# Gate and up projections of a hybrid decoder step as seven half products per pair of tiles, down projection in two parts

## Chip, cores and metric

The kernel runs on one NeuronCore of a Trainium2 chip. The core's engines are TensorE (PE, with its weight loads PEld), VectorE (DVE), ScalarE (ACT), GpSimd (POOL) and SyncE (SP, which issues the DMAs). The metric is the device time of one execution in microseconds.

## The reference

One inference step of a one-layer decoder: 512 prompt tokens and 8 sequences of 8 sampled tokens, 576 tokens together, 1,024 features. Two groups of token mixers (a state space model and an RWKV-7 recurrence) are followed by an output projection, then by the part that the change concerns, and by a per-layer embedding:

```
hf = rmsnorm(h, w['norm_ffn'])
h = h + (jax.nn.silu(hf @ w['w_gate']) * (hf @ w['w_up'])) @ w['w_down']
gate = jax.nn.sigmoid(rmsnorm(h, w['norm_ple']) @ w['w_ple_gate'])
h = h + gate * (p.astype(h.dtype) @ w['w_ple_proj'])
```

`rmsnorm` divides each token's row by its root mean square and multiplies by a weight per feature. The inner width D_FF is 2,816, which is 22 tiles of 128. All inputs are float32.

## The kernel before

Everything is kept transposed: features on the 128 partitions, the 576 tokens along the free dimension. `hs[c]` (c from 0 to 7) are the eight tiles of the residual h, each 128 x 576.

*Matmuls in three parts.* A float32 product is made from the faster format float32r: every operand is split into hi (a copy rounded by ScalarE, line 92 in `act`) and lo (the rest, a subtraction), and hi*hi + hi*lo + lo*hi is accumulated in PSUM (`mm3`, lines 208 to 212). `split` (line 177) does it for activations, `wsplit` (line 186) for weights; the subtractions go to GpSimd and VectorE in turn (line 195 for weights, line 183 for activations), unless `lo_eng` names an engine. One PSUM bank holds 512 columns, so a tile of 576 tokens is done in two halves of 288 (`HV`). `linear(xs, ps)` (line 214) loads the weights of one output tile in blocks of up to four k tiles (128 x 512, 256 KB, tag raw with three buffers), splits them and issues six matmuls per k tile. `lin_bank` hands out PSUM tiles of two banks from two pools with two tiles each.

*Order of the work.* The program lists the operations in order; a scheduler with a timeline of its own decides, per engine, in which order they are queued: the earlier in the program the higher the priority, but what is not ready in that timeline lets others go ahead. Each engine then runs its queue strictly in that order.

*Feed-forward stage (lines 1282 to 1312).* `after` (line 1251) multiplies each tile of h by the norm's weight, splits it into the operand `XF` (buffers xhi and xlo, eight of each), and adds up the squares. The normalisation by token, `rs` (128 x 576), comes from `rstd_of` (line 1262): sums over features by matmuls with a column of ones (line 306), square root and reciprocal, transposes on TensorE (line 312) and a copy by ScalarE. For each of the 22 inner tiles f, `linear` makes gate and up; line 1298 multiplies gate by rs, ScalarE applies Silu, line 1303 multiplies by up, and the result is split into `AF2[f]` (tags ah0 to ah21 and al0 to al21, one buffer each), lo on GpSimd. The factor rs of up is left out there and applied behind the down projection: for each of eight tiles of h, line 1308 makes the down product over all 22 inner tiles, line 1310 multiplies by rs on VectorE, line 1311 adds to h on GpSimd, and `after` prepares the next stage's operand and squares.

*Last stage (lines 1317 to 1363).* The per-layer gate (8 tiles, weights WP split once and kept) in two token ranges of 320 and 256 columns, its product with the embedding part `PL` (loaded from DRAM, `pl`), the addition to h and the final norm. WP and PL live in the buffers of `AF2`, whose tags they use.

## Time and profile before

| | us |
|---|---|
| median of the runs (3, from 1414.13 to 1415.24) | 1415.04 |
| the profiled execution | 1409.36 |
| its span, from the first to the last instruction | 1407.6 |
| token mixers and output projection, 0 to about 911 | 911 |
| gate and up, about 911 to 1195 | 284 |
| down, about 1195 to 1334 | 139 |
| per-layer gate and final norm, about 1334 to the end | 74 |

TensorE's mean granted clock over the span is 0.936 of full speed. In the rows of groups that follow, the fields are line, engine, operation, output<-inputs, shape and count, then busy time in us and the mean of one in ns, then the idle time of the engine just before them with what ended it. In timeline rows the first two numbers are start and length in us, and the bracket gives the idle time before and its releaser. In rows of stretches the columns are start and end, length, busy us (and instructions) of PE, PEld, DVE, ACT and POOL, the granted TensorE clock, and the share and GB/s of the DMA engines.

### The profile page before, as it was taken

The page shows a single profiled execution, that of the slowest core. Times are in us where ns is not written, and L with a number is a line of the kernel's source. Part 1 is how long each engine was busy: PE and PEld are TensorE (multiplying, and loading weights), DVE is VectorE, ACT ScalarE, POOL GpSimd, SP SyncE. Part 2 cuts the span into 40 slices and gives each one's busy share as a digit, 9 for nine tenths or more (in the row PEclk, how much of TensorE's full clock was granted, in tenths as well). Part 3 has the DMA queues.
Part 4 walks back from the last instruction along what each step waited for, and adds up shares of the span by engine and source line. Part 5 has one row for each costly group of instructions (what it writes and reads, how often), then busy time and mean ns, then how long its engine had stood idle before and what let it go on. Part 6 is the DMA issues. An engine that isn't in the chain of part 4 may idle for free.

```text
span 1407.6 us, 24774 instructions
## 1 busy us (share of the span) xinstructions
PE 1278.4 (91%) x9761; PEld 1188.2 (84%) x9761; DVE 721.8 (51%) x1335; ACT 590.8 (42%) x1186; POOL 565.4 (40%) x552
## 2 busy tenths in 40 slices
PE   6887999899889988969869987999999999999996
PEld 5786897788678967956748877999999999999996
DVE  6648658696777766845265574422222221122255
ACT  6564436544653464334534353332333333222253
POOL 4345515632543334123346574523332333344432
PEclk9998999999999988957969997999999999999998
DMA  4322233234223412342514541223233323332432
GB/s 157 128 56 81 73 109 99 68 92 119 61 84 86 114 50 88 117 117 101 194 64 140 179 127 45 84 82 83 83 83 83 83 83 83 83 82 82 126 109 68
DMA packets 94452, 135.46 MB, mean 96 GB/s; under 512 B 34704, under 2 KB 39056, under 8 KB 94336
## 3 DMA queue, kind: packets, MB, share of 16 engines
q1 hardware_dynamic: 94336, 133.88, 32.2%
q8 instruction: 77, 1.26, 0.4%
q14 instruction: 39, 0.32, 0.1%
HBM read 106.10 MB, written 27.75 MB: 95 GB/s over the span
## 4 chain that ended last, share of the span: by engine, by line
PE 67%; DVE 18%; DMA 5%; ACT 4%; issue 4%; POOL 1%; SPq 1%; DVEq 0%; ACTq 0%; POOLq 0%
PE lin L210 17%; PE lin L212 17%; PE lin L211 16%; PE lin L578 2%; DVE Tt L638 2%; DVE tmp L636 2%; DVE h L367 1%; DVE wlo L195 1%; PE y L1157 1%; PE lin L225 1%; DVE suv L787 1%; PE lin L1334 1%; DVE bk L556 1%; PE cx L756 1%; PE lin L1335 1%
## 5 line engine op out<-in xcount | busy, mean ns | idle before, releaser
L210 PE MATMUL lin<-xhi,whi 128*128 128x288 f32 (+1 forms) x1488 | 448.2, 301 | 5.2 <-ACT xhi L92 2.5
L212 PE MATMUL lin<-xhi,wlo 128*128 128x288 f32 (+1 forms) x1488 | 446.9, 300 | 5.2 <-DVE wlo L195 3.6
L211 PE MATMUL lin<-xlo,whi 128*128 128x288 f32 (+1 forms) x1488 | 444.6, 299 | 0.0
L195 POOL TENSOR_TENSOR wlo<-raw,whi 128x512 fp32r<-128x512 f32 (+1 forms) x136 | 179.8, 1322 | 435.4 <-ACT whi L92 421.9
L92 ACT ACTIVATE whi<-raw 128x512 fp32r<-128x512 f32 (+1 forms) x272 | 169.1, 622 | 407.1 <-PE lin L211 339.4
L212 PEld LDWEIGHTS lin<-xhi,wlo 128*128 128x128 f32 (+1 forms) x1488 | 281.6, 189 | 11.6 <-DVE wlo L195 6.0
L210 PEld LDWEIGHTS lin<-xhi,whi 128*128 128x128 f32 (+1 forms) x1488 | 280.9, 189 | 11.0 <-ACT whi L92 3.5
L211 PEld LDWEIGHTS lin<-xlo,whi 128*128 128x128 f32 (+1 forms) x1488 | 280.9, 189 | 2.9 <-issue 1.0
L195 DVE TENSOR_TENSOR wlo<-raw,whi 128x512 fp32r<-128x512 f32 (+1 forms) x136 | 96.4, 709 | 162.4 <-ACT whi L92 159.5
L212 PE MATMUL lin<-ah,wlo 128*128 128x288 f32 x352 | 103.9, 295 | 0.3
L210 PE MATMUL lin<-ah,whi 128*128 128x288 f32 x352 | 104.1, 296 | 0.0
L211 PE MATMUL lin<-al,whi 128*128 128x288 f32 x352 | 103.8, 295 | 0.0
L212 PEld LDWEIGHTS lin<-ah,wlo 128*128 128x128 f32 x352 | 66.3, 188 | 1.0 <-POOL wlo L195 1.0
L211 PEld LDWEIGHTS lin<-al,whi 128*128 128x128 f32 x352 | 66.1, 188 | 0.0
L210 PEld LDWEIGHTS lin<-ah,whi 128*128 128x128 f32 x352 | 66.0, 187 | 0.0
L1303 DVE TENSOR_TENSOR sg<-lin,sg 128x576 f32<-128x576 f32 x22 | 16.7, 758 | 83.3 <-PE lin L212 82.1
L1298 DVE TENSOR_TENSOR sg<-lin,rstd 128x576 f32<-128x576 f32 x22 | 16.7, 757 | 74.1 <-PE lin L212 70.9
L638 DVE TENSOR_TENSOR Tt<-Tt,tmp 72x30 f32<-72x30 f32 (+14 forms) x120 | 45.9, 383 | 3.3
L636 DVE TENSOR_TENSOR tmp<-L,Tt 72x30 f32<-72x30 f32 (+14 forms) x120 | 45.7, 381 | 3.2
L210 PE MATMUL lin<-xu,whi 128*128 128x288 f32 x128 | 39.8, 312 | 8.3 <-ACT xu L92 6.6
L212 PE MATMUL lin<-xu,wlo 128*128 128x288 f32 x128 | 39.7, 312 | 7.2 <-DVE wlo L195 5.5
L183 POOL TENSOR_TENSOR al<-sg,ah 128x576 fp32r<-128x576 f32 x22 | 31.5, 1432 | 35.1 <-ACT ah L92 35.1
(368 smaller groups left out, 2607.2 us busy)
## 6 DMA issues: line engine op xcount, KB each, us to landing
raw<-wts SPq DMA_DIRECT2D x271, 256.0 KB, 2.7
S<-s_wkv SPq DMA_DIRECT2D x8, 512.0 KB
hd<-s_ssm SPq DMA_DIRECT2D x8, 512.0 KB, 4.0
o_ssm_s<-hd SPq DMA_DIRECT2D x8, 512.0 KB, 3.1
xbc_d<-E SPq DMA_DIRECT2D x12, 288.0 KB, 2.1
x<-xT SPq DMA_DIRECT2D x8, 288.0 KB, 6.0
gate_d<-g SPq DMA_DIRECT2D x8, 288.0 KB, 3.3
bv_d<-bv SPq DMA_DIRECT2D x8, 288.0 KB, 2.1
```

The lines of the kernel that those rows point to most:

```text
L92: S.activation(out, in_, func, bias=bias, scale=scale)
L183: eng.tensor_tensor(lo[:], src, hi[:].bitcast(F32), ALU.subtract)
L195: eng.tensor_tensor(lo[:, 0:n], raw[:, 0:n], hi[:, 0:n].bitcast(F32), ALU.subtract)
L210: T.matmul(ps[:, a:b], whi, xhi[:, a:b], start=first, stop=False)
L211: T.matmul(ps[:, a:b], whi, xlo[:, a:b], start=False, stop=False)
L212: T.matmul(ps[:, a:b], wlo, xhi[:, a:b], start=False, stop=last)
L225: T.matmul(ps[:, a:b], w, x[:, a:b], start=True, stop=True)
L578: T.matmul(ps[:, c:c + 256], s.BK[jj][:, g].rearrange("p a t -> p (a t)"), s.G[:, g, jj].rearrange("p a e t -> p (a e t)"), start=True, st ...
L636: V.tensor_tensor(o, L[:, jx:jx + 1, jx + 1:32].to_broadcast([NB, jx, n]), Tt[:, 0:jx, jx:jx + 1].to_broadcast([NB, jx, n]), ALU.mult)
L638: V.tensor_tensor(Tt[:, 0:jx, jx + 1:32], Tt[:, 0:jx, jx + 1:32], o, ALU.subtract)
L1298: V.tensor_tensor(s_[:], ps, rs[:], ALU.mult)
L1303: V.tensor_tensor(s_[:], up, s_[:], ALU.mult)
```

## The change

The two products of the first two inner tiles stay as they were, except that the result is multiplied by rs at once. For all others h is normalised first (`xn`, with rs) and the product of a pair of output tiles is written as a 2 x 2 block product: the weights in blocks a11, a12 (first output tile, k tiles 0 to 3 and 4 to 7) and a21, a22 (second output tile), the operand in blocks b11, b12 (k tiles 0 to 3, columns 0 to 287 and 288 to 575) and b21, b22 (k tiles 4 to 7). With sums and differences of blocks (Winograd's form of Strassen's identity) four output blocks need seven products of blocks:

```
s1 = a21+a22   s2 = s1-a11   s3 = a11-a21   s4 = a12-s2
T1 = b12-b11   T2 = b22-T1   T3 = b22-b12   T4 = b21-T2
p1 = a11 b11   u = p1 + s2 T2   v = u + s3 T3
c11 = p1 + a12 b21   c12 = u + s1 T1 + s4 b22
c21 = v + a22 T4     c22 = v + s1 T1
```

A half product is 4 k tiles x 3 matmuls of 288 columns. The seven operands are split once, before the first pair; the weights, as blocks or as sums of blocks, are split for each half product (`wh` and `wl`, four buffers each, shared with `xn`). The inner tiles are finished with rs in them, so the down projection needs no factor; it runs in two parts, over the first 12 inner tiles behind pair 5 and over the other 10 at the end, each added to h by VectorE. `AF2` has ten or twelve entries at a time: four in buffers of their own, the others in xhi and xlo. WP and PL get a pool of their own (`f2`). The constant RS1 goes. The weights are packed in the new order.

```diff
--- before.py
+++ after.py
@@ -21,6 +21,7 @@
 HALF = 288
 KT = D // P
 NFF = 22
+NSPLIT = 6
 C_DECAY = math.exp(-0.5)
 EPS = 1e-6
 GN_EPS = 64e-5
@@ -42,7 +43,6 @@
 G0AT = 5
 RA = 2
 SEQ = "zzszzszszspyw"
-RS1 = 1
 RS2 = 1
 NPART = SEQ.count("w")
 SQP = (3,)
@@ -1274,42 +1274,147 @@
             linear(YS, ps)
             V.tensor_tensor(hs[c][:], ps, hs[c][:], ALU.add)
         after(c, hs[c], "norm_ffn", me, "xs", 8, st)
-    if not RS1:
-        rs = rstd_of(st)
     mix2.close()
 
 
     fp = ctx.enter_context(tc.tile_pool(name="fp", bufs=1, reuse_waits="tile"))
     lins.append(ctx.enter_context(tc.tile_pool(name="lin2", bufs=2, space=PSUM, reuse_waits="tile")))
+    cm_ = ExitStack()
+    cm = cm_.enter_context(tc.tile_pool(name="cm", bufs=1, side="right", reuse_waits="tile"))
+    NP = NFF // 2
 
     def ft(name, bufs=9):
         return fp.tile([P, NT], F32, tag="f", name=nm(name), bufs=bufs)
 
+    AF2 = []
+
+    def inner(src, eng):
+
+        if len(AF2) < 4:
+            AF2.append(split(src, fp, (f"ah{len(AF2)}", f"al{len(AF2)}"), [P, NT], lo_eng=eng))
+        else:
+            AF2.append(split(src, xp, ("xhi", "xlo"), [P, NT], lo_eng=eng))
+
+
     XF = st["x"]
-    AF2 = []
-    for f in range(NFF):
+    for f in range(2):
         ps = lin_ps()
         linear(XF, ps)
-        if f == 0 and RS1:
-            up = lin_ps()
-            linear(XF, up)
+        up = lin_ps()
+        linear(XF, up)
+        if f == 0:
             rs = rstd_of(st)
         s_ = ft("sg")
         V.tensor_tensor(s_[:], ps, rs[:], ALU.mult)
         act(s_[:], s_[:], AF.Silu)
-        if f or not RS1:
-            up = lin_ps()
-            linear(XF, up)
         V.tensor_tensor(s_[:], up, s_[:], ALU.mult)
-        AF2.append(split(s_[:], fp, (f"ah{f}", f"al{f}"), [P, NT], lo_eng=G))
+        V.tensor_tensor(s_[:], s_[:], rs[:], ALU.mult)
+        inner(s_[:], G)
+
+
+    OPS = {n: tuple(cm.tile([P, 4, HALF], F32R, tag=f"{n}{p}", name=nm(n)) for p in "hl")
+           for n in ("B11", "T2", "T1", "T3", "B21", "T4", "B22")}
+    xn = [cm.tile([P, NT], F32, tag=("wh", "wl")[k // 4], name=nm("xn"), bufs=4) for k in range(KT)]
+    for k in range(4):
+        for c in (k, k + 4):
+            V.scalar_tensor_tensor(xn[c][:], hs[c][:], par("norm_ffn", c), rs[:], ALU.mult, ALU.mult)
+        b11, b12 = (xn[k][:, a:b] for a, b in HV)
+        b21, b22 = (xn[k + 4][:, a:b] for a, b in HV)
+        t = ft("tt")
+        t3, t2 = (t[:, a:b] for a, b in HV)
+
+        def parts(n, src):
+            split(src, None, (None, None), None, hi=OPS[n][0][:, k], lo=OPS[n][1][:, k])
+
+        parts("B11", b11)
+        V.tensor_tensor(t3, b22, b12, ALU.subtract)
+        V.tensor_tensor(b12, b12, b11, ALU.subtract)
+        V.tensor_tensor(t2, b22, b12, ALU.subtract)
+        parts("T2", t2)
+        parts("T1", b12)
+        parts("T3", t3)
+        parts("B21", b21)
+        V.tensor_tensor(b21, b21, t2, ALU.subtract)
+        parts("T4", b21)
+        parts("B22", b22)
+
+    nraw = [0]
+
+    def quarter():
+
+        nraw[0] += 1
+        pool, tag = ((wp, "raw"), (cm, "raw2"))[nraw[0] % 2]
+        t = pool.tile([P, 512], F32, tag=tag, name=nm("raw"), bufs=3)
+        nc.sync.dma_start(t[:], A["wts"][wat[0]:wat[0] + P * 512].rearrange("(p n) -> p n", p=P))
+        wat[0] += P * 512
+        return t
+
+    def half_product(ps, w, n, first):
+        hi, lo = split(w[:], cm, ("wh", "wl"), [P, 512], bufs=4)
+        xh, xl = OPS[n]
+        for k in range(4):
+            wh, wl = (t[:, k * P:(k + 1) * P] for t in (hi, lo))
+            T.matmul(ps, wh, xh[:, k], start=first and k == 0, stop=False, skip_group_check=True)
+            T.matmul(ps, wh, xl[:, k], start=False, stop=False, skip_group_check=True)
+            T.matmul(ps, wl, xh[:, k], start=False, stop=k == 3, skip_group_check=True)
+
+    def two_tiles(p1, ps1, ps2, ps3):
+
+        a11, a21, a22, a12 = (quarter() for _ in range(4))
+        s1, s2 = (cm.tile([P, 512], F32, tag="sw", name=nm("sw"), bufs=3) for _ in range(2))
+        half_product(ps1, a11, "B11", True)
+        act(p1, ps1)
+        V.tensor_tensor(s1[:], a21[:], a22[:], ALU.add)
+        V.tensor_tensor(s2[:], s1[:], a11[:], ALU.subtract)
+        ca, cb = ft("ca"), ft("cb")
+        c12, c21, c22 = ca[:, HALF:NT], cb[:, 0:HALF], cb[:, HALF:NT]
+        half_product(ps2, s2, "T2", True)
+        V.tensor_tensor(c12, ps2, p1, ALU.add)
+        half_product(ps3, s1, "T1", True)
+        G.tensor_tensor(a21[:], a11[:], a21[:], ALU.subtract)
+        half_product(ps2, a21, "T3", False)
+        V.tensor_tensor(c22, ps2, p1, ALU.add)
+        V.tensor_tensor(c22, ps3, c22, ALU.add)
+        half_product(ps1, a12, "B21", False)
+        half_product(ps2, a22, "T4", False)
+        V.tensor_tensor(c21, ps2, p1, ALU.add)
+        V.tensor_tensor(s2[:], a12[:], s2[:], ALU.subtract)
+        half_product(ps3, s2, "B22", False)
+        V.tensor_tensor(c12, ps3, c12, ALU.add)
+        return ca, cb
+
+    def inner_pair():
+        b1, b3 = lin_bank(), lin_bank()
+        p1 = ft("p1")
+        ga, gb = two_tiles(p1[:, 0:HALF], b1[:, 0:HALF], b1[:, 512:512 + HALF], b3[:, 0:HALF])
+        act(ga[:, 0:HALF], b1[:, 0:HALF], AF.Silu)
+        act(ga[:, HALF:NT], ga[:, HALF:NT], AF.Silu)
+        act(gb[:], gb[:], AF.Silu)
+        b2 = lin_bank()
+        ua, ub = two_tiles(p1[:, HALF:NT], b2[:, 0:HALF], b2[:, 512:512 + HALF], b3[:, 512:512 + HALF])
+        V.tensor_tensor(ga[:, 0:HALF], b2[:, 0:HALF], ga[:, 0:HALF], ALU.mult)
+        G.tensor_tensor(gb[:], ub[:], gb[:], ALU.mult)
+        V.tensor_tensor(ga[:, HALF:NT], ua[:, HALF:NT], ga[:, HALF:NT], ALU.mult)
+        inner(gb[:], G)
+        inner(ga[:], V)
+
+    def down(last):
+        for c in range(8):
+            ps = lin_ps()
+            linear(AF2, ps)
+            V.tensor_tensor(hs[c][:], ps, hs[c][:], ALU.add)
+            if last:
+                after(c, hs[c], "norm_ple", fp, "f", 9, st)
+        AF2.clear()
+
+    for p in range(1, NP):
+        inner_pair()
+        if p == NSPLIT - 1:
+            down(False)
+    cm_.close()
+    f2 = ctx.enter_context(tc.tile_pool(name="f2", bufs=1, side="right", reuse_waits="tile"))
     st = {"x": []}
-    for c in range(8):
-        ps = lin_ps()
-        linear(AF2, ps)
-        t = ft("dn")
-        V.tensor_tensor(t[:], ps, rs[:], ALU.mult)
-        G.tensor_tensor(hs[c][:], hs[c][:], t[:], ALU.add)
-        after(c, hs[c], "norm_ple", fp, "f", 9, st)
+    down(True)
     if not RS2:
         rs = rstd_of(st)
 
@@ -1317,7 +1422,7 @@
     XF = st["x"]
     WP, PL = [], []
     for c in range(8):
-        pl = fp.tile([P, NT], F32, tag=f"a{'hl'[c // 6]}{16 + c % 6}", name=nm("pl"))
+        pl = f2.tile([P, NT], F32, tag=f"pl{c}", name=nm("pl"))
         nc.sync.dma_start(pl[:], pp_d[c][:])
         PL.append(pl)
     for a, b in ((0, 320), (320, NT)):
@@ -1325,7 +1430,7 @@
         acc = None
         for c in range(8):
             if a == 0:
-                WP.append([wload(4, *(fp.tile([P, 512], F32R, tag=f"a{p}{2 * c + i}", name=nm("wp")) for p in "hl"))
+                WP.append([wload(4, *(f2.tile([P, 512], F32R, tag=f"w{p}{2 * c + i}", name=nm("wp")) for p in "hl"))
                            for i in range(2)])
             ps = lin_bank()[:, 0:n]
             for k in range(KT):
@@ -1442,11 +1547,21 @@
     wos = np.concatenate([wo[14 * P:16 * P], wo[:8 * P]])
     for c in range(8):
         put_tile(wos if c < NPART else wo, 0, 10 if c < NPART else 8, c)
-    for c in range(NFF):
-        put_tile(wg, 0, 8, c)
-        put_tile(wu, 0, 8, c)
-    for c in range(8):
-        put_tile(wd, 0, NFF, c)
+    lo4, hi4 = list(range(4)), list(range(4, 8))
+    for c in range(0, NFF, 2):
+        for i, w in ((0, wg), (0, wu), (1, wg), (1, wu)) if c == 0 else ():
+            put_tile(w, 0, 8, i)
+        for w in (wg, wu) if c else ():
+            put(w, lo4, c)
+            put(w, lo4, c + 1)
+            put(w, hi4, c + 1)
+            put(w, hi4, c)
+        if c // 2 in (NSPLIT - 1, NFF // 2 - 1):
+            k0 = 0 if c // 2 == NSPLIT - 1 else 2 * NSPLIT
+            ks = [k0 + (k if k0 == 0 and k < 2 else k ^ 1) for k in range(c + 2 - k0)]
+            for m in range(8):
+                for k in range(0, len(ks), 4):
+                    put(wd, ks[k:k + 4], m)
     for c in range(8):
         put_tile(wpg, 0, 8, c)
     out["wts"] = np.concatenate(blocks)
```

## The prediction

> **What bounds the kernel now.** I read the page's first lines, then the table of stretches, then the groups of instructions by shape over the last 500 us, and last the timelines of single engines at the places that the change touches. The page says that TensorE is the busy engine:
>
> ```profile
> span 1407.6 us, 24774 instructions
> PE 1278.4 (91%) x9761; PEld 1188.2 (84%) x9761; DVE 721.8 (51%) x1335; ACT 590.8 (42%) x1186; POOL 565.4 (40%) x552
> ```
>
> In the stage that the change rewrites, TensorE is the only limit. The columns are the stretch, its length, the busy time of PE, PEld, DVE, ACT and POOL, and the granted clock:
>
> ```profile
> 911.00:1195.00 284.00, 284.00 (x2135) 284.00 (x2134) 62.99 (x91) 88.31 (x136) 87.76 (x66) 1.00 0.30 83
> 1195.00:1334.00 139.00, 138.71 (x1036) 138.01 (x1036) 28.47 (x41) 37.35 (x63) 56.47 (x43) 1.00 0.31 87
> ```
>
> Gate and up (the first row) and down (the second) keep TensorE without a gap at full clock, and VectorE and GpSimd are busy less than a third of the first stretch. So time goes only by taking matmuls away, or comes by making TensorE wait. What one matmul is worth is read from the beat of the multiplication by rstd, once per tile of gate:
>
> ```profile
> 923.86 0.76 DVE L1298 TENSOR_TENSOR sg<-lin,rstd 128x576 f32<-128x576 f32 x1 [3.16 <-ACT rstd L92]
> 929.57 0.76 DVE L1298 TENSOR_TENSOR sg<-lin,rstd 128x576 f32<-128x576 f32 x1 [1.93 <-PE lin L212]
> 936.04 0.76 DVE L1303 TENSOR_TENSOR sg<-lin,sg 128x576 f32<-128x576 f32 x1 [5.71 <-PE lin L212]
> 942.37 0.76 DVE L1298 TENSOR_TENSOR sg<-lin,rstd 128x576 f32<-128x576 f32 x1 [4.97 <-PE lin L212]
> ```
>
> From 929.57 to 942.37 are 12.80 us for 96 matmuls of 288 columns: 133.3 ns each.
>
> **Matmuls removed.** Tiles 2 to 21 become ten pairs, each with a gate and an up product. A product of two tiles costs 7 half products of 12 matmuls instead of 8: 20 x 12 = 240 fewer, 240 x 133.3 ns = **-32.0 us**. A half product lasts 1.6 us, a pair 168 x 133.3 ns = 22.4 us (before 25.6). The down projection keeps its 1,056 matmuls in two parts. Weight bytes are the same.
>
> **What feeds them.** Every half product needs its weights split into hi (ScalarE) and lo (VectorE and GpSimd in turn), so a pair takes 14 splits where two tiles took 8, and block sums come on top. Prices:
>
> ```profile
> L195 DVE TENSOR_TENSOR wlo<-raw,whi 128x512 fp32r<-128x512 f32 x65 | 44.7, 688 | 107.7 <-ACT whi L92 107.6
> L195 POOL TENSOR_TENSOR wlo<-raw,whi 128x512 fp32r<-128x512 f32 x65 | 85.5, 1315 | 220.4 <-ACT whi L92 211.0 <-PE lin L312 9.4
> L183 POOL TENSOR_TENSOR al<-sg,ah 128x576 fp32r<-128x576 f32 x22 | 31.5, 1432 | 35.1 <-ACT ah L92 35.1
> L92 ACT ACTIVATE whi<-raw 128x512 fp32r<-128x512 f32 x129 | 81.6, 633 | 260.1 <-PE lin L211 227.8 <-POOL al L183 19.2 <-issue 12.5
> L1345 DVE TENSOR_TENSOR h<-h,pg 128x320 f32<-128x320 f32 x8 | 3.9, 491 | 0.2
> L1345 DVE TENSOR_TENSOR h<-h,pg 128x256 f32<-128x256 f32 x8 | 3.4, 425 | 0.3
> L1342 DVE TENSOR_TENSOR pg<-lin,rstd 128x320 f32<-128x320 f32 x8 | 3.9, 484 | 1.3 <-ACT rstd L92 1.3
> L1342 DVE TENSOR_TENSOR pg<-lin,rstd 128x256 f32<-128x256 f32 x8 | 3.3, 415 | 0.0
> L1351 POOL TENSOR_TENSOR sq<-sq,sq 128x320 f32<-128x320 f32 x6 | 5.5, 922 | 6.9 <-ACT sq L92 6.9
> L1351 POOL TENSOR_TENSOR sq<-sq,sq 128x256 f32<-128x256 f32 x6 | 4.4, 734 | 11.2 <-ACT sq L92 9.8 <-issue 1.5
> L324 DVE SCALAR_TENSOR_TENSOR x<-x,pv,rstd x8: 804/812/1984, 30.4 to 39.2; 128x576 f32<-128x576 f32 x8
> ```
>
> Half tiles of 288 columns lie midway between 256 and 320: 0.458 us on VectorE, 0.45 with an input from PSUM, 0.828 on GpSimd. Taken alone no engine is full. ScalarE has 14 x 0.633 = 8.9 us of hi copies and a few copies and Silus per 22.4 us. But VectorE and GpSimd are not alone. Three rows of one moment of the down stage, start and length first:
>
> ```profile
> 1301.70 1.44 POOL L1259 TENSOR_TENSOR hsq<-hsq,hsq 128x576 f32<-128x576 f32 x1 [0.80 <-ACT hsq L92]
> 1302.23 1.52 DVE L183 TENSOR_TENSOR xlo<-hg,xhi 128x576 fp32r<-128x576 f32 x1 [0.77 <-ACT xhi L92]
> 1303.09 1.81 POOL L195 TENSOR_TENSOR wlo<-raw,whi 128x512 fp32r<-128x512 f32 x1
> ```
>
> VectorE's subtraction from two SBUF tiles begins under a GpSimd operation and ends at 1303.75, 0.61 us after GpSimd's end (1303.14); the next GpSimd operation then ends 1.15 us after that (1304.90), where its mean is 1.315. The two take turns, and a handover hides about 0.15 us. The multiplications of the beat above, whose one input is PSUM, took 0.76 us every time.
>
> The Trainium skill, page "SBUF — State Buffer", section "Who interferes with whom", says the same as a rule: a VectorE instruction with two SBUF inputs and a GpSimd instruction that reads SBUF exclude each other for the whole instruction, one with at most one SBUF input goes free. The trace agrees (0.61 us behind the other's end). It speaks against this change, which moves the work from TensorE to just these two engines; without the rule the next two parts would come to 10.8 and about 2 us instead of 17 and 12.
>
> **Before the first pair.** Operands B11 to B22 need rstd, and rstd comes late:
>
> ```profile
> 915.20 1.17 PE L306 MATMUL lin<-ones,hsq 128*128 128x1 f32 x10
> 922.43 0.71 PE L312 MATMUL lin<-ident,rn 128*128 128x128 f32 x5
> 923.18 0.65 ACT L92 ACTIVATE rstd<-lin 128x576 f32<-128x576 f32 x1
> ```
>
> The sums over tokens run at 915.2, the transposes only at 922.4 behind the up product of tile 0; the new code has them in the same place. So the preparation starts at 923.9, and TensorE has work of tile 1 until 936.0. VectorE: 6 operations of the first two tiles (4.5 us; 3.0 of it from PSUM), 8 multiplications by the norm at 0.81 (6.5), 16 subtractions (7.3) and 14 lo parts (6.4) of 0.458, two weight parts (1.4): 26.1 us. GpSimd: 14 lo parts of 0.828 (11.6), two activation parts (2.9), three weight parts (3.9): 18.4. In turns: 26.1 + 18.4 - 3.0 beside PSUM work - 38 handovers x 0.15 = 35.8 us. The first half product needs B11 of the last k, some 5.5 us ahead of the end: 954.2. TensorE can do three quarters of that product earlier, so it waits from 937.2: 17.0 us. If nothing excluded anything, VectorE's 26.1 us alone, with the last operand 4.0 ahead of the end (946.0), would make it 8.8. I take 15, nearer to the rows of the turns, as some weight and activation parts may be queued later. After an idle PE the clock falls; this is the join behind the down stage, two stretches and the one after:
>
> ```profile
> 1342.00:1344.00 2.00, 2.00 (x9) 2.00 (x9) 0.68 (x2) 1.78 (x4) 0.81 (x1) 0.50 0.58 146
> 1346.00:1348.00 2.00, 2.00 (x10) 1.96 (x10) 0.69 (x1) 0.64 (x2) 0.00 (x0) 0.50 0.68 200
> 1348.00:1350.00 2.00, 2.00 (x15) 2.00 (x14) 0.49 (x1) 1.98 (x3) 1.15 (x1) 0.95 0.43 133
> ```
>
> Half clock for about 7 us costs up to 3.5 us; I take 2. Sum: **+17 us**, ends 8.8 and 20.5.
>
> **In the ten pairs.** GpSimd per pair: 7 weight parts and 2 block differences (9 x 1.315 = 11.8), the product for gb and its lo part (2.9): 14.7 us. VectorE with two SBUF inputs: 7 weight parts and 6 block sums (13 x 0.688 = 8.9), lo of ga 0.76, one half product 0.46: 10.2. Together 24.9 us strictly in turns, 21.0 with 26 handovers of 0.15, against 22.4 us of matmuls: the shared way into SBUF is 94% full at best. Eleven VectorE operations from PSUM (4.9 us) fit beside GpSimd. Two waits are new in each two-tile product: the fourth half product accumulates on ps2 only after VectorE has read it for c12, the sixth only after c22, and each has one half product, 1.6 us, as cover. VectorE runs in order: behind a GpSimd operation (up to 1.3), its own (0.69) and the read (0.45) that is up to 2.5 us, 0.9 late. Twice in each of 20 products gives 0 to 1.8; I take a third of it, 0.6: **+12 us**. Ends: 0, and 25 if the pair takes 24.9.
>
> **Edits at nothing.** The first down part starts with tiles that are long ready; the tiles of the last pair come only in its third weight block, 8 tiles x 6 matmuls = 6.4 us or more later, which covers the last additions, products and splits (about 4 us by the rows above; uncovered, that much twice). Its eight additions to h have 72 x 133.3 ns = 9.6 us each. Weight DMAs have six raw buffers and the same order.
>
> **Join to the last stage.** Before, after the last down matmul (about 1334):
>
> ```profile
> 1334.23 0.76 DVE L1310 TENSOR_TENSOR dn<-lin,rstd 128x576 f32<-128x576 f32 x1 [3.05 <-PE lin L212]
> 1335.07 1.44 POOL L1311 TENSOR_TENSOR h<-h,dn 128x576 f32<-128x576 f32 x1 [0.94 <-DVE dn L1310]
> 1332.67 6.96 DMA raw<-wts
> 1339.65 0.63 ACT L92 ACTIVATE wp<-raw 128x512 fp32r<-128x512 f32 x1 [2.44 <-DMA raw<-wts]
> 1340.19 0.67 ACT L92 ACTIVATE xhi<-hg 128x576 fp32r<-128x576 f32 x1
> 1340.34 0.42 PE L1334 MATMUL lin<-xhi,wp 128*128 128x320 f32 x1 [1.75 <-ACT wp L92]
> ```
>
> A weight load took 7 us, since the loads of pl waited for tiles of the down stage and came at the same time; ScalarE waited for it ahead of xhi; TensorE idled 1.75 us and then ran the half clock shown. Now pl and the weights have tiles of their own, so the loads can come early, and the GpSimd addition (1.44) is gone. Against that, six of the eight xhi buffers hold down operands until the last down tile has read them, so the splits for c = 2 and up crowd into its last 4 us. Gone entirely, idle and half clock are worth 5.3; I take **-4 us**, ends -5.5 and 0.
>
> **Sum:** -32 + 17 + 12 - 4 = -7 us. The profiled execution took 1409.4 us around its 1407.6 us span and would take 1402.4; the runs' median, 1415.0, is 5.7 above it, and the forecast is 1408.0.
>
> **Rivals.** *The shared way sets the beat (slower).* One mechanism: VectorE and GpSimd exclude each other without hidden handovers, the pair takes 24.9 us, and the preparation stands at its upper end. For it speaks that 24.9 is the sum of the durations as they are; against it the 0.15 us of the rows shown. Time: -32 + 20.5 + 25 - 3 = +10.5, 1425.5. It decides from 24.3 us per pair (-32 + 17 - 4 = -19, 1.9 per pair). Chance 0.22.
>
> *The turns are hidden (faster).* Weight buffers four deep let lo parts run 4.8 us ahead, the reads are in time, preparation 8.8 + 2: -32 + 10.8 + 2 - 4 = -23.2, 1391.8. Against it: 94%. Chance 0.11.
>
> *ScalarE stands behind TensorE.* The copy of ps1 to p1 waits for the first half product; if the next weights' hi copy is queued behind it, the second half product waits for copy (0.5), hi (0.63) and lo (1.3), 2.4 us, 20 times 48 instead of 12: +29, 1444. Against it: the order on ScalarE is not that of the code, as weights pass results:
>
> ```profile
> 926.28 0.63 ACT L92 ACTIVATE whi<-raw 128x512 fp32r<-128x512 f32 x1 [0.45 <-ACT sg L92]
> 926.82 0.67 ACT L92 ACTIVATE ah<-sg 128x576 fp32r<-128x576 f32 x1
> ```
>
> Here a weight copy goes ahead of the finished product of the tile before. Chance 0.04.
>
> **How the numbers follow.** The forecast's mechanism has the rest, 0.63; of it 0.50 ends faster and 0.13 within 0.2% (2.8 us, about what a measurement of this kernel can tell from no change). Faster: 0.50 + 0.11 = 0.61; slower: 0.22 + 0.04 = 0.26. The range goes from just under the faster rival to the slower one, 1388 to 1426; outside it lie the third rival and the far ends of the others, under 0.2.
>
> **What would show it.** Right: 9,521 matmuls; a TensorE gap of about 15 us behind tile 1, followed by half clock; gaps below 1 us at the fourth and sixth half products, released by VectorE; pairs of 23.6 us; VectorE subtractions above 1 us and GpSimd above 1.6 where they meet; no idle at the join. The forecast is wrong if pairs take 22.5 us (the faster rival) or over 24.3, or if the gaps are released by ScalarE or by a DMA.

## The result, and the profile after

The changed kernel takes 1498.16 us (median of 4 runs, 1496.36 to 1499.45), the kernel before 1414.59 us (4 runs, 1413.52 to 1415.24): 1.0591 times as long, 95% interval 1.0572 to 1.0609. The forecast was 1408.0 us and faster; it was wrong in sign and far outside its range. The page's first lines after:

```profile
span 1497.2 us, 24845 instructions
PE 1298.0 (87%) x9521; PEld 1193.1 (80%) x9521; DVE 896.9 (60%) x1563; ACT 643.0 (43%) x1304; POOL 654.6 (44%) x608
```

The 240 matmuls are gone (9,521). VectorE has 175 us more work, GpSimd 89, and TensorE's busy time even grew: behind the long waits shown below its matmuls start 0.24 us apart in place of 0.13. The profiled execution took 1498.93 us.

The stages ahead of the feed-forward stage (FFN) are the same program, but their time differs from one execution to the next. Two stretches there, before and then after (the last three columns are the granted clock, DMA share and GB/s):

```profile
300.00:450.00 150.00, 133.60 (x1103) 121.22 (x1103) 110.71 (x230) 73.35 (x169) 63.30 (x69) 0.94 0.31 90
450.00:600.00 150.00, 139.35 (x1119) 124.57 (x1117) 110.81 (x238) 71.14 (x160) 49.43 (x51) 0.92 0.31 90
```

```profile
300.00:450.00 150.00, 133.57 (x1062) 120.88 (x1061) 106.34 (x221) 72.32 (x167) 61.83 (x68) 0.91 0.29 87
450.00:600.00 150.00, 140.30 (x1090) 124.42 (x1090) 107.81 (x222) 68.55 (x155) 49.35 (x51) 0.89 0.28 85
```

With a clock 0.03 lower there, the first FFN matmul came at 918.48 us instead of 908.54. That is no part of the change, so traces are compared below from that matmul to the end: 499.1 us before, 578.7 after, 79.6 us more. This leaves out a spread of 14 us: in the 16 traces of this case the same stages put that matmul between 907.20 and 921.36 us. Each such figure still comes from one trace.

Where the 79.6 us come from, by TensorE's timeline (a matmul at 133.3 ns):

| part | after, us | at 133.3 ns a matmul | lost |
|---|---|---|---|
| two plain tiles, to the first half product (963.84) | 45.4 | 25.6 | 19.8 |
| first two-tile product | 23.2 | 11.2 | 12.0 |
| the other 19 products and both down parts, to the last down matmul's end (1422.23) | 435.2 | 353.6 | 81.6 |
| last down matmul to the end | 75.0 | (73.4 before) | 1.6 |

Together 115.0 lost. Before, the first FFN matmul to the last of down took 425.6 us, 35.2 more than the 390.4 of the third column: the 32.0 of the removed matmuls, and 3.2 of small gaps and of the last stage's first matmuls, which run among the last of down in both kernels and are in the 81.6 as well. So the pairs (but for the first product) and the down parts lost about 78 us. Some 49 of these are waits of TensorE, the rest is mostly matmuls at a lower clock. The table of waits of TensorE from the FFN on says which waits these are (total us, times, longest):

```profile
PE lin L1357 <- DVE ca L1372: 34.2, 17, 3.9
PE lin L1357 <- ACT wh L92: 10.0, 2, 9.2
PE lin L1357 <- DVE cb L1376: 9.4, 17, 0.6
PE lin L212 <- DVE wlo L195: 6.4, 1, 6.4
PE lin L1357 <- DVE ca L1383: 5.4, 5, 2.7
PE lin L1359 <- POOL wl L183: 4.9, 2, 4.2
```

The first and third are the two reads that the forecast named, c12 (line 1372) and c22 (line 1376). They are late in nearly every product, c12 by up to 3.9 us. One of the long ones, at the start of a pair; VectorE's and GpSimd's rows, then TensorE's:

```profile
1260.87 1.77 DVE L1368 TENSOR_TENSOR sw<-sw,raw 128x512 f32<-128x512 f32 x1
1262.04 1.89 POOL L1396 TENSOR_TENSOR cb<-cb,cb 128x576 f32<-128x576 f32 x1
1262.56 1.92 DVE L183 TENSOR_TENSOR wl<-raw,wh 128x512 fp32r<-128x512 f32 x1
1263.89 1.71 POOL L183 TENSOR_TENSOR wl<-raw,wh 128x512 fp32r<-128x512 f32 x1
1264.40 1.52 DVE L1397 TENSOR_TENSOR ca<-ca,ca 128x288 f32<-128x288 f32 x1
1266.67 0.76 DVE L183 TENSOR_TENSOR al<-ca,ah 128x576 fp32r<-128x576 f32 x1 [0.75 <-ACT ah L92]
1267.35 0.69 DVE L183 TENSOR_TENSOR wl<-raw,wh 128x512 fp32r<-128x512 f32 x1
1267.95 0.45 DVE L1372 TENSOR_TENSOR ca<-lin,p 128x288 f32<-128x288 f32 x1
1268.45 0.61 PE L1357 MATMUL lin<-T,wh 128*128 128x288 f32 x1 [3.68 <-DVE ca L1372]
```

The VectorE operations that meet a GpSimd one end just behind it: the low part at 1264.48 behind 1263.93, the half tile at 1265.92 behind 1265.60. What costs 0.69 or 0.45 alone costs 1.5 to 1.9 here. The read that TensorE waits for takes 0.45 us and stands last in this queue. Then the clock falls (column before the last two):

```profile
1266.00:1268.00 2.00, 0.00 (x0) 0.00 (x0) 1.33 (x3) 2.00 (x4) 0.19 (x1) 1.00 0.64 221
1268.00:1270.00 2.00, 1.55 (x6) 1.55 (x7) 0.40 (x2) 0.25 (x1) 2.00 (x2) 0.60 0.40 132
1270.00:1272.00 2.00, 1.70 (x8) 1.35 (x6) 0.26 (x1) 0.45 (x1) 0.55 (x1) 0.54 0.02 8
```

The order on TensorE differs from the code's: T2 and T1 are exchanged, so the half products run B11, T1, T2, T3, B21, T4, B22. The product with T2 writes ps2, which lies in the same PSUM tile as ps1, and waits for ScalarE's copy of ps1 to p1; T1 writes ps3 in another tile and is put ahead. So T3 follows T2 directly, and the read of c12 between them has no half product as cover: in products without a long wait it begins only when T2 ends, and TensorE waits 0.62 us for it. In the same way B21, which accumulates on ps1, waits for the read of ps2 for c22 (0.55 us each time).

The preparation, first VectorE and GpSimd, then TensorE's waits and the one of ScalarE:

```profile
934.48 9.12 DVE L1320 SCALAR_TENSOR_TENSOR xn<-h,pv,rstd 128x576 f32<-128x576 f32 x8
944.78 1.27 DVE L195 TENSOR_TENSOR wlo<-raw,whi 128x512 fp32r<-128x512 f32 x1
950.38 10.64 POOL L183 TENSOR_TENSOR T<-tt,T 128x288 fp32r<-128x288 f32 x2 [3.18 <-ACT T L92]
964.20 0.80 POOL L183 TENSOR_TENSOR T<-tt,T 128x288 fp32r<-128x288 f32 x1 [0.32 <-ACT T L92]
967.09 1.76 POOL L183 TENSOR_TENSOR T<-xn,T 128x288 fp32r<-128x288 f32 x2 [0.39 <-ACT T L92]
```

```profile
946.11 0.61 PE L212 MATMUL lin<-xhi,wlo 128*128 128x288 f32 x1 [6.38 <-DVE wlo L195]
963.84 0.61 PE L1357 MATMUL lin<-B,wh 128*128 128x288 f32 x1 [9.18 <-ACT wh L92]
970.57 0.61 PE L1359 MATMUL lin<-B,wl 128*128 128x288 f32 x1 [4.17 <-POOL wl L183]
```

```profile
963.16 0.63 ACT L92 ACTIVATE wh<-raw 128x512 fp32r<-128x512 f32 x1 [7.33 <-POOL T L183]
```

Eight multiplications by the norm stand in VectorE's queue ahead of a low part of tile 1, so the plain tile itself waits 6.38 us. Two of GpSimd's low parts took 10.64 us (7.10 and 3.58) under VectorE's almost unbroken row of two-input operations; the same operation took 0.80 us when VectorE stood still. And the weights' hi copy waited 7.33 us for GpSimd's low parts, since it needs a buffer that held normalised tiles. The last operand is done at 968.85.

### The profile page after: what moved, and what is told of

Read it like the earlier page. It is cut to its first block, busy times and chain, and to the rows that moved or that the text cites. A ratio compares the mean times of both kernels' runs of the same rounds, so it can differ in the third digit from the quotient of the medians.

```text
span 1497.2 us, 24845 instructions
## 1 busy us (share of the span) xinstructions
PE 1298.0 (87%) x9521; PEld 1193.1 (80%) x9521; DVE 896.9 (60%) x1563; ACT 643.0 (43%) x1304; POOL 654.6 (44%) x608
## 5 line engine op out<-in xcount | busy, mean ns | idle before, releaser
L212 PE MATMUL lin<-xhi,wlo 128*128 128x288 f32 (+1 forms) x1072 | 326.9, 305 | 12.9 <-DVE wlo L195 11.1
L210 PE MATMUL lin<-xhi,whi 128*128 128x288 f32 (+1 forms) x1072 | 327.1, 305 | 4.9 <-ACT xhi L92 2.2
L211 PE MATMUL lin<-xlo,whi 128*128 128x288 f32 (+1 forms) x1072 | 324.5, 303 | 0.1
L212 PEld LDWEIGHTS lin<-xhi,wlo 128*128 128x128 f32 (+1 forms) x1072 | 205.5, 192 | 20.0 <-DVE wlo L195 13.9
L210 PEld LDWEIGHTS lin<-xhi,whi 128*128 128x128 f32 (+1 forms) x1072 | 204.8, 191 | 10.7 <-ACT whi L92 3.5
L211 PEld LDWEIGHTS lin<-xlo,whi 128*128 128x128 f32 (+1 forms) x1072 | 204.9, 191 | 3.0 <-issue 1.0
L1357 PE MATMUL lin<-T,wh 128*128 128x288 f32 x320 | 104.1, 325 | 40.4 <-DVE ca L1372 34.2
L1358 PE MATMUL lin<-T,wh 128*128 128x288 f32 x320 | 101.3, 317 | 0.0
L1359 PE MATMUL lin<-T,wl 128*128 128x288 f32 x320 | 100.6, 316 | 0.7 <-POOL wl L183 0.7
L1357 PE MATMUL lin<-B,wh 128*128 128x288 f32 x240 | 76.7, 320 | 18.6 <-DVE cb L1376 9.4
L1359 PE MATMUL lin<-B,wl 128*128 128x288 f32 x240 | 74.1, 309 | 4.2 <-POOL wl L183 4.2
L1358 PE MATMUL lin<-B,wh 128*128 128x288 f32 x240 | 74.1, 309 | 0.0
L92 ACT ACTIVATE wh<-sw 128x512 fp32r<-128x512 f32 x60 | 37.6, 628 | 73.3 <-PE lin L1358 69.3
```

Source lines behind the costliest of these rows:

```text
L92: S.activation(out, in_, func, bias=bias, scale=scale)
L210: T.matmul(ps[:, a:b], whi, xhi[:, a:b], start=first, stop=False)
L211: T.matmul(ps[:, a:b], whi, xlo[:, a:b], start=False, stop=False)
L212: T.matmul(ps[:, a:b], wlo, xhi[:, a:b], start=False, stop=last)
L1357: T.matmul(ps, wh, xh[:, k], start=first and k == 0, stop=False, skip_group_check=True)
L1358: T.matmul(ps, wh, xl[:, k], start=False, stop=False, skip_group_check=True)
```

## The experiments

Theory after this trace: two causes in the pairs, PSUM tiles that hold two accumulators, and VectorE and GpSimd in each other's way; and a preparation of its own. In all tables and texts, "a pair" is 168 matmuls at the rate of the stretch shown (length x 168 / count). Each ratio is to runs of the kernel before in the same batch, with its 95% interval.

**e1: each accumulator in a PSUM tile that nothing else waits on.**

```
-        b1, b3 = lin_bank(), lin_bank()
+        b1, bB, b3 = lin_bank(), lin_bank(), lin_bank()
...
-        ... two_tiles(p1[:, 0:HALF], b1[:, 0:HALF], b1[:, 512:512 + HALF], b3[:, 0:HALF])
+        ... two_tiles(p1[:, 0:HALF], b1[:, 0:HALF], bB[:, 0:HALF], b3[:, 0:HALF])
...
-        ... two_tiles(p1[:, HALF:NT], b2[:, 0:HALF], b2[:, 512:512 + HALF], b3[:, 512:512 + HALF])
+        ... two_tiles(p1[:, HALF:NT], b2[:, 0:HALF], bB[:, 512:512 + HALF], b3[:, 512:512 + HALF])
```

> Edit: ps1, ps2 and ps3 of a two-tile product lie in three PSUM tiles of their own; in the changed kernel ps1 and ps2 are two banks of one tile. Theory (dependencies are kept per PSUM tile): the wait of B21 for VectorE's c22 (0.55 us) goes, since B21 writes ps1 and c22 reads ps2; T1 no longer jumps ahead of T2, so each read of ps2 has another half product as cover and the 0.6 us in front of T3 goes. 20 x 1.15 = 23 us, and of the 3.7 us in front of T3 at each pair's start 1.6 us are covered too, so that the clock falls less: 1498 - 45 = about 1453 (1435 to 1475). Rival (the waits are true dependencies, or VectorE is simply late): nothing moves, 1490 to 1498.

Measured: 1458.48 us (1.0315 times before, 1.0269 to 1.0362), FFN to end 534.4, 44.3 less: as the theory said. The order is now B11, T2, T1, B21, T3, the next product's B11, T4, B22.

**e2: GpSimd's weight low parts written as zeros**, on the changed kernel; half of the weights' low parts are left out.

> Edit: in the ten pairs GpSimd's half of the weight lo parts is a fill with zero in place of a subtraction (the lo part of every other half product is left out); VectorE's queue keeps its operations. Theory (VectorE with two SBUF inputs and GpSimd reading SBUF exclude each other): VectorE's weight lo parts and block sums fall from means of 1.0 to 1.3 us to 0.69, and the wait of T3 for c12 at each pair's start falls from 3.2 to 3.8 us to about 0.6, without half clock behind it: 9 pairs x 6.5 = about -58, so 1440 (1430 to 1455). The 0.55 and 0.6 us waits inside stay. Rival (VectorE's own work and its order make it late): those waits stay above 2.5 us and the time stays above 1480.

Measured: 1478.09 us (1.0457, 1.038 to 1.0533). Between the two: the waits at the pair's start fell from 3.2 to 3.9 us to about 2.2, the waits of 0.55 and 0.62 us stayed.

**e3: four plain tiles ahead of the identity in place of two.**

> Edit: four inner tiles instead of two are done the old way ahead of the pairs (nine pairs instead of ten). Theory (the preparation of the seven operands has too little cover): the 25.6 us of tiles 2 and 3 hide it; the gaps ahead of and inside the first pair (6.4 + 9.2 + 0.9 + 4.2 us and the half clock behind them, some 25 us in all) shrink to under 8, and one pair of 32 us becomes 25.6: 1498 - 18 - 6 = 1474 (1465 to 1482). Rival (VectorE's row of operations keeps GpSimd out whatever the cover, and the stall only moves): only the pair counts, 1488 to 1494.

Measured: 1488.23 us (1.0512, 1.0451 to 1.0573), by the rival: more TensorE work beside the preparation hides little of it (the first product still took 26.7 us).

**e4: eight quarter products, the identity undone, the rest of the change kept.**

> Edit: only the block identity is undone. The operand is normalised first as in the changed kernel, the weights come in the same blocks and order, the down projection has its two parts and the last stage its own buffers, but each pair is made of eight quarter products with two output tiles in PSUM, without sums of blocks. Theory (identity's extra VectorE and GpSimd work makes the loss): no gap inside the pairs, 25.6 us each; a shorter preparation costs 5 to 12 us, the join gives back 3 to 4: 1415 + 5 = 1420 (1412 to 1430). Rival (normalising first, two down parts or the new buffers cost by themselves): 1440 or more.

Measured: 1430.13 us (1.0117, 1.0073 to 1.0162), FFN to end 510.0. That is just above the theory's range (1412 to 1430), and TensorE has no wait above 0.2 us in the pairs. So the identity costs 68 us of the 83.6, and what comes with it (normalised operands, two down parts) 11 to 15. The trace of e4 shows one wait of 4.23 us in the preparation and two of 2.0 and 1.94 at the join to the last stage.

**e5: e1 with e2's zeros.**

> The run with own PSUM tiles, with every low part of a weight that fell to GpSimd (half of them) written as zeros, so that GpSimd reads nothing for it: half of the low parts are left out of the products. Theory, VectorE and GpSimd work in exclusive turns and that is what is left of the waits in the pairs (about 3 us a pair in the run with own tiles, at a period of 26.7 us): VectorE's low parts and sums fall to 0.7 us, the pairs to 22.6 to 23.2 us, the time to 1422 us (1415 to 1432). Rival, the chain of dependent reads keeps the waits whoever fills the low parts: pairs above 25.5 us, 1445 to 1456 us.

**e6: e1, with all two-input work of the pairs on VectorE.**

```
-        hi, lo = split(w[:], cm, ("wh", "wl"), [P, 512], bufs=4)
+        hi, lo = split(w[:], cm, ("wh", "wl"), [P, 512], lo_eng=V, bufs=4)
...
-        G.tensor_tensor(a21[:], a11[:], a21[:], ALU.subtract)
+        V.tensor_tensor(a21[:], a11[:], a21[:], ALU.subtract)
...
-        G.tensor_tensor(gb[:], ub[:], gb[:], ALU.mult)
+        V.tensor_tensor(gb[:], ub[:], gb[:], ALU.mult)
...
-        inner(gb[:], G)
+        inner(gb[:], V)
```

> Own PSUM tiles, and all two-input work of the ten pairs on VectorE: 14 low parts, 8 sums of weights, 10 sums of outputs, products and low parts of the inner tiles; GpSimd idle in the pairs. Theory, the two engines can't work at once on such operations and GpSimd is only the slower of two users of one way: with 14 x 0.69 + 8 x 0.68 + 10 x 0.45 + about 4 us = 23.7 us of VectorE a pair and none of it lengthened, pairs of 24 to 25 us, 1435 us (1425 to 1448). Rival, GpSimd does carry a share beside VectorE: VectorE's 20.3 us a pair grow by the moved work to about 28 to 30 us, and the time to 1475 to 1505 us.

Measured: e5 1429.89 us (1.0105, 1.0048 to 1.0162), e6 1414.38 us (0.9997, 0.9963 to 1.0032). e5 is in its theory's range, with pairs slightly longer than forecast; e6 is faster than both its theory and its rival. **e9: e6 without the own tiles**, so that the two causes stand in all four combinations.

> The changed kernel with its PSUM tiles as they are, and all two-input work of the ten pairs on VectorE. With own PSUM tiles the same step took the time from 1458.5 to 1414.4 us. Theory, the exclusive turns cause the waits of 3.2 to 3.8 us at each pair's start, and the shared PSUM tile costs only the two uncovered reads in each product (0.62 and 0.55 us of wait, some 0.15 us more each until TensorE runs on): 20 products x 1.5 us = 30 us above the run with own tiles and VectorE alone, 1444 us (1436 to 1450). Rival, the two causes simply add, so that own tiles are again worth 40 us: 1454 us (1451 to 1462). A third, the shared tile is the whole of it: 1480 us or more.

Measured: e9 1463.04 us (1.035, 1.0305 to 1.0395). The pairs of the second down part, one stretch from each trace (PE, PEld, DVE, ACT, POOL, clock), in the order after, e1, e9, e5, e6:

```profile
1206.00:1330.00 124.00, 101.88 (x678) 97.25 (x677) 75.22 (x102) 46.48 (x83) 61.23 (x44) 0.93 0.23 66
```

```profile
1185.00:1295.00 110.00, 97.62 (x695) 93.62 (x695) 84.35 (x109) 49.18 (x88) 68.72 (x47) 0.99 0.26 77
```

```profile
1188.00:1298.00 110.00, 94.63 (x666) 89.27 (x666) 79.92 (x144) 46.45 (x84) 0.00 (x0) 1.00 0.25 72
```

```profile
1170.00:1265.00 95.00, 91.22 (x680) 90.50 (x679) 67.08 (x102) 47.39 (x84) 39.82 (x44) 1.00 0.31 89
```

```profile
1168.00:1260.00 92.00, 91.34 (x680) 90.44 (x679) 82.32 (x149) 47.93 (x85) 0.00 (x0) 1.00 0.29 90
```

| run | own PSUM tiles | GpSimd in the pairs | a pair, us | FFN to end, us |
|---|---|---|---|---|
| after | no | yes | 30.7 | 578.7 |
| e1 | yes | yes | 26.6 | 534.4 |
| e9 | no | no | 27.7 | 544.3 |
| e5 | yes | yes, its weight low parts as fills | 23.5 | 509.9 |
| e6 | yes | no | 22.7 | 497.9 |

Own tiles are worth 44.3 us with GpSimd and 46.4 without, GpSimd's absence 34.4 and 36.5: the causes simply add, and my guess for e9 that the shared tile would then cost 30 us fell (the time lies just above even the range for plain adding, 1451 to 1462). In e6 the longest wait of TensorE in the pairs is this one:

```profile
PE lin L1357 <- DVE cb L1380: 1.1, 4, 0.3
```

The surprise is in VectorE's column: in e6 it does 149 operations in 92 us, in e1 109 in 110 us, and a pair keeps it busy for 20.3 us in e6 (82.32 x 22.7 / 92) and for 20.4 in e1 (84.35 x 26.6 / 110). Taking on GpSimd's share cost it nothing. I had forecast 23.7 us for e6 by adding up lengths, but operations 0.68 long follow each other every 0.60 us there. The same kind of low part after (the whole FFN) and in e6 (the stretch of 92 us), busy us and mean ns:

```profile
L183 DVE TENSOR_TENSOR wl<-raw,wh 128x512 fp32r<-128x512 f32 x40 | 44.3, 1108 | 3.3 <-ACT wh L92 3.3
```

```profile
L183 DVE TENSOR_TENSOR wl<-raw,wh 128x512 fp32r<-128x512 f32 x32 | 21.5, 684 | 0.5
```

**The preparation.** e6 still lost some 26 us there (first half product 44.9 us behind the first FFN matmul, first product 17.9 us). e7 is e1, e8 is e1 with four plain tiles, both with the operands' low parts on VectorE and the normalised tiles in buffers of the FFN's general pool:

```
-    xn = [cm.tile([P, NT], F32, tag=("wh", "wl")[k // 4], name=nm("xn"), bufs=4) for k in range(KT)]
+    xn = [None] * KT
...
+            xn[c] = ft("xn")
...
-            split(src, None, (None, None), None, hi=OPS[n][0][:, k], lo=OPS[n][1][:, k])
+            split(src, None, (None, None), None, lo_eng=V, hi=OPS[n][0][:, k], lo=OPS[n][1][:, k])
```

> Own PSUM tiles, the eight normalised tiles in buffers of the FFN's general pool, not in those of the weight parts, and all low parts of the operands on VectorE, none on GpSimd. Theory, the preparation was long because weight parts waited for buffers that held normalised tiles and because GpSimd was kept out for some 10 us: the first half product starts 35 us or less behind the first matmul of the FFN (45.4 before), no wait for a weight's high part above 2 us, time 1444 us (1436 to 1451). Rival, VectorE's sum of work in the preparation (about 28 us) sets it whoever does the low parts: first half product 42 us or more behind the first matmul or the same loss inside the first product, 1452 to 1462 us.

> The last run with four plain tiles ahead of the identity in place of two (one pair less, +3.2 us of matmuls). Theory: 25.6 us more of TensorE's work lie over the preparation, all of it is covered, TensorE waits less than 3 us between the last plain matmul and the end of the first two-tile product: nine pairs at 26.7 us, 1438 us (1430 to 1446). Rival, the preparation isn't covered since the plain tiles' own low parts stand in the same queue: 1450 to 1460 us.

Measured: e7 1455.84 us (1.028, 1.0226 to 1.0333), e8 1448.01 us (1.0222, 1.0172 to 1.0271). The first half product of e7 starts 27.9 us behind the first matmul, as the theory said, but the loss moved into the first product, which now takes 38 us: the rival was right. e8 lies between its theory's range and its rival's. e10 and e11 are the same two steps on e6, with the plain tiles' low parts on VectorE as well:

> Own PSUM tiles, the pairs' two-input work on VectorE alone, and the preparation as well: the low parts of the operands, of the two plain tiles and of their weights on VectorE, the normalised tiles in buffers of the FFN's general pool. Theory, VectorE's sum sets the preparation, about 35 us from the reciprocal root on, against 24 us of TensorE's work (two plain products and the first two-tile product): a loss of 11 to 14 us where the run with VectorE alone in the pairs still lost about 31: 1397 us (1390 to 1406). Rival, the order of VectorE's queue keeps the first product stretched as in the run with the preparation on VectorE: 1410 to 1418 us.

> The last run with four plain tiles ahead of the identity: one pair less (3.2 us of matmuls more), about 47 us of VectorE from the reciprocal root on against 49 us of TensorE's work. Theory: the preparation costs 2 to 6 us, 1393 us (1385 to 1401), which would be under the kernel before. Rival, the plain tiles' work on VectorE stands ahead of the operands, so that the cover grows no faster than the work: 1400 to 1412 us.

Measured: e10 1413.01 us (0.9982, 0.9948 to 1.0016), e11 1417.33 us (1.0016, 0.9989 to 1.0043). e10 came out by its rival, e11 above even its rival's range (1400 to 1412). VectorE in e11 while the plain tiles run, and then in the first product:

```profile
936.00:960.00 24.00, 24.00 (x182) 24.00 (x181) 12.35 (x18) 9.69 (x15) 0.00 (x0) 1.00 0.27 78
972.00:990.00 18.00, 8.63 (x24) 5.71 (x24) 18.00 (x42) 8.04 (x19) 0.00 (x0) 0.64 0.00 0
```

VectorE is half idle beside the plain tiles and full afterwards: the preparation stands behind all plain tiles in its queue, and its first multiplication starts at 964.69, 28 us after rstd. So e12 writes the preparation into the loop over the plain tiles, one of its four steps behind each; e13 puts two steps behind the second tile and none behind the last, and e14 has two plain tiles with two steps each. The edit of e13 (e12 and e14 differ from it in PREP, e14 also in the number of plain tiles):

```
+PREP = ((0,), (1, 2), (3,), ())
...
-    for k in range(4):
+    def prep(k):
...
         inner(s_[:], V)
+        for k in PREP[f]:
+            prep(k)
```

> The run with VectorE alone, own PSUM tiles and four plain tiles, with the preparation written into the loop over the plain tiles, one of its four steps behind each plain tile, so that it stands in VectorE's queue from the second plain tile on. In the run without this, VectorE was busy for 18 of the 30 us after the reciprocal root and then full for 30 us, in which the first two-tile product took 34 us in place of 11.2. Theory, that order is what kept the preparation from being covered: the first product takes 13 to 17 us, the time falls by about 18 us, to 1399 us (1392 to 1406), under the kernel before by 1%. Rival, VectorE's sum (some 47 us from the reciprocal root to the end of the first product's sums) is the bound and no order helps: above 1410 us.

> As the run before it, with steps two and three of the preparation both behind the second plain tile, the last behind the third and none behind the fourth. Theory: VectorE has the operands ready before the last plain product ends, the first two-tile product takes 12 to 14 us, 1397 us (1390 to 1404). Rival, the earlier steps delay the plain tiles' low parts by as much: the same time as the run before it or longer.

> The same order with two plain tiles, two steps of the preparation behind each. Theory: the cover is too short by about 11 us (35 us of VectorE, 24 us of TensorE), so the order brings little here: 1410 us (1404 to 1415). Rival, order alone is the cause: 1398 us or less.

Measured: e12 1404.36 us (0.9928, 0.9893 to 0.9963), e13 1402.70 us (0.9924, 0.9889 to 0.9959), e14 1413.07 us (1.0002, 0.9964 to 1.004). All three are in their theories' ranges, but e12 and e13 can't be told apart (FFN to end 487.1 and 486.3). VectorE in e13 beside the plain tiles and in the first product:

```profile
934.00:958.00 24.00, 22.47 (x163) 21.53 (x162) 24.00 (x49) 15.33 (x33) 0.00 (x0) 1.00 0.19 65
970.00:984.00 14.00, 12.91 (x97) 12.68 (x97) 13.16 (x24) 7.15 (x13) 0.00 (x0) 1.00 0.37 113
```

With the order right, four plain tiles do cover most of the preparation: from the first FFN matmul to the end of the first product e13 takes 69.3 us and e11 84.0, where the matmuls alone are 62.4. With two plain tiles the cover is too short, and the order brings nothing: FFN to end 497.2 in e14, 498.1 in e10. e13 beats the kernel before by 0.8% with nine identity pairs: FFN to end 486.3 us against 499.1. Its margin is that of a median of 12 runs that reach from 1393.40 to 1408.05, against 1402.68 to 1422.46 for before.

## Why the prediction was wrong, point by point

- **Matmuls removed, -32.0: right.** 9,521, and in e6 a pair costs 22.7 us against the 22.4 of its matmuls alone.
- **In the ten pairs, +12: this step failed; it measured about 78.** The sentence that fell is "each has one half product, 1.6 us, as cover". I took the order of the code for TensorE's order and looked at data alone. The waits are kept for whole PSUM tiles: ps1 and ps2 share one, so T2 waited for the copy of ps1, T1 was moved ahead of it, and the cover of c12 was gone; B21 waited for a read of ps2 that it has nothing to do with. Own tiles took back 39 of the 78 (44.3 from FFN to end), GpSimd's absence another 34, which leaves about 5 in e6.
- **The turns.** The mechanism was right and my sum of it wrong: 21.0 to 24.9 us of turns for 22.4 us of matmuls was read as "94% full", a mean. At a pair's end the products, low parts and sums of both engines come together, the read stands behind all of them, and TensorE waits 3.2 to 3.9 us and then runs at half clock for a while. The slower rival had this mechanism, but its 24.9 us a pair was too cheap: with own tiles the turns still make 26.6. I also counted GpSimd as help. e6 shows that it was none: without it VectorE's 82.3 us of 92 contain everything and no wait is above 0.3 us. The Trainium skill, page "Perfetto Trace Analysis", section "Optimizing Scalar/DVE Operations", warns that moving work between VectorE and GpSimd might not help, as they share a read port; here the trace agrees and goes further, since moving it back is worth 36.5 us.
- **Before the first pair, +17: mis-sized, it measured 31.8.** The preparation itself was as long as forecast, 35 us (933.81 to 968.85) against 35.8. What failed is the path from it to TensorE. The forecast let TensorE do three quarters of the first half product early and then wait for B11 until 954.2, 45.7 us behind before's first FFN matmul at 908.54. In the trace the half product only began 45.4 us behind the first FFN matmul, and it had waited for a weight's hi copy, whose buffer held a normalised tile. That the two times agree is luck: in e7, with other buffers and all low parts on VectorE, it begins at 27.9. What I left out is what follows: "The first half product needs B11 of the last k, some 5.5 us ahead of the end" counts one operand, but that product's other operands and weights were not ready either, and it took 23.2 us in place of 11.2. Both the length of VectorE's work and its place matter: with four plain tiles e11 and e13 do the same work and differ by 17.6 us from FFN to end, with two (e10, e14) the place changes nothing.
- **Join, -4: not there, +1.6.** The same last part took 70.4 to 74.6 us in the traces of the experiments, so 1.6 is no clear loss; but the gain is missing. TensorE waits at the join for the new rstd, where before it waited 1.75 us for a weight:

```profile
1435.60 1.30 PE L312 MATMUL lin<-ident,rn 128*128 128x128 f32 x5 [2.71 <-DVE rn L309]
1438.40 0.63 PE L1439 MATMUL lin<-xhi,wp 128*128 128x320 f32 x1 [1.50 <-ACT rstd L92]
```

e4 has the two waits as well (2.0 and 1.94), so they don't come from the identity. Beyond that no run took this join apart; that the loads no longer matter is only read from these rows.

- **ScalarE behind TensorE:** not seen in the pairs; its two waits (10.0 us) are in the preparation, the long one for the buffer named above.

## What to carry to other kernels

A cover counted in half products holds only for the order in which the engine really gets them: look up what shares a PSUM tile with the accumulator before trusting it, since a wait can be for a neighbour. Where VectorE and GpSimd both work from SBUF, price the work on VectorE alone first; the second engine can make both slower than one. Work that must be hidden needs a cover that is long enough and has to stand in the queue beside it: a longer cover alone (e11) brought nothing, the right place alone (e14) brought nothing, both together (e13) took about 11 us off.

## What the runs showed of the hardware

- GpSimd can be kept out for long: two operations that take 0.80 us each when VectorE stands still took 7.10 and 3.58 us while VectorE ran two-input operations almost without a break. The Trainium skill, page "SBUF — State Buffer", section "Who interferes with whom", says that such a VectorE instruction and a GpSimd instruction that reads SBUF contend, and the trace agrees. The turns at the pair's start look fair, this moment does not.
- Waits of 2.2 us, with some of about 0.6 us around them, can be enough for half clock. In the changed kernel, behind the waits of 3.23 to 3.89 us at the pairs' starts, matmuls always ran at half pace (0.24 us apart). In e2 these waits are 2.20 to 2.22 us, and behind five of the seven the clock was at half as well; one of the five, and then one of the two others:

```profile
1030.00:1034.00 4.00, 3.45 (x15) 3.10 (x14) 1.51 (x3) 0.63 (x1) 0.00 (x0) 0.50 0.13 49
1222.00:1226.00 4.00, 3.45 (x24) 3.21 (x25) 1.51 (x3) 0.63 (x1) 0.00 (x0) 1.00 0.29 68
```

In e9 a wait of 1.65 us once a pair, with shorter ones between, left it at 1.00 throughout. Shorter waits can add up: in e10 no wait of the first product was above 2.0 us, but TensorE was busy for 4.66 of 8 us and had half clock:

```profile
950.00:958.00 8.00, 4.66 (x12) 3.02 (x12) 8.00 (x19) 4.12 (x10) 0.00 (x0) 0.50 0.00 0
```

The Trainium skill, page "TensorE: Matmul & The Clock Gate", section "HAM oscillation — how this bites in real kernels", gives an idle gap of about 3.4 us as the limit. The waits of e2 and e10 were shorter, so it was no safe limit here, and the measurement decides.
- The same instructions ahead of the FFN ran with a granted clock of 0.94 or 0.91 in one stretch, and the kernel before spread from 1402.68 to 1422.46 us over 29 runs. A gain below 1% needs many runs, or a comparison from a point in the trace behind that stage.
